# Memory attention of the prompt as two passes of seven Strassen products on pairs of tiles

## The chip, the cores and the metric

The program runs on one core of one Trainium2 chip. A core has TensorE (PE in the profile; the loading of its weights is listed as PEld), VectorE (DVE), ScalarE (ACT), GpSimd (POOL) and SyncE (SP), which issues most of the DMAs. Each engine takes its own instructions in order, and waits on semaphores for the others. The metric is device time in microseconds, the median of several runs: lower is better.

## The reference, cut to what matters

One layer of a streaming encoder. For the prompt (2048 rows of 1024 channels, float32) it does a mixer, then attention into 256 memory tokens, then a SwiGLU feed-forward. The middle one is what changes:

```python
def memory_attention(h, mk, mv, w_mq, w_mo):          # h = rmsnorm(x, g_mem_pre)
    q = (h @ w_mq).reshape(B, T, MEM_HEADS, MEM_HEAD_DIM)          # 4 heads of 256
    s = jnp.einsum("bthd,bmhd->bhtm", q, mk, ...) * (MEM_HEAD_DIM ** -0.5)
    p = jax.nn.softmax(s, axis=-1)
    o = jnp.einsum("bhtm,bmhd->bthd", p.astype(mv.dtype), mv).reshape(B, T, D_MODEL)
    return o @ w_mo
# x = x + rmsnorm(memory_attention(...), g_mem_post), then h = rmsnorm(x, g_ffn_pre)
```

The kernel folds the weights into the memory first: F1 = w_mq times the keys (1024 x 1024, its columns head by head) and F2 = values times w_mo (1024 x 1024). The attention of a row is then two products with 1024 x 1024 matrices, h F1 = scores and p F2 = output, with the softmax between them.

## The kernel before

Rows are worked in tiles of 128: prompt tiles 0 to 15, and tile 16 (`S_TILE`), the sample rows. The program is five stages, one after the other:

- `phase_mem`: norm of the memory tokens, keys and values, then F1 and F2, which are kept in DRAM (`f1s`, `f2s`).
- the projections, the convolution and the band attention (`phase_proj`, `attention`), which the change doesn't touch.
- `mixout`: output projection of the mixer, row tile by row tile, with memory attention of the sample rows (`cross_sample`) in between. The sum with the residual goes to DRAM as `x1[t]` (an addition on POOL, L1038, and a DMA that POOL issues, L1039).
- `phase_cross` (L1169): memory attention of the prompt.
- `gate_up` and `down`: the feed-forward, as seven Strassen products of 2 x 2 blocks. Row tiles are taken in pairs, whose seven row forms (sums and differences of half rows) lie in DRAM as `hn[g]`; `tform` loads and transposes them.

float32 products are made of three passes on PE: each operand is split into hi (rounded to fp32r, on ACT) and lo (the rest, on DVE or POOL), and hi·hi + hi·lo + lo·hi is summed. `mm3` issues the three passes for one bank of PSUM (512 columns), `mm3h` for two.

In `phase_cross` every tile t goes through `norm` (square sum on ACT, power on POOL, scaling on DVE, 8 transposes on PE, split), `scores` (8 blocks x 3 passes x 2 halves = 48 matmuls of 512 columns, then maximum, exponential, normalization), `probs` (8 transposes and the split of the probabilities) and `values` (48 matmuls, then `postnorm`). F1 and F2 are loaded and split once, at the start (`load`), and stay in SBUF. The loop interleaves `probs(t)`, `scores(t+1)`, `norm(t+2)`, `values(t)`. `natural(g, p)` reads two finished tiles back from `x2`, norms them and writes their seven row forms to `hn`; it runs from the fifth tile on, and for the last two pairs (`todo`) in `gate_up`.

The order of instructions on each engine is fixed when the program is built, by a scheduler that goes by its own estimate of durations, so what the text writes next to each other may stand apart on the engines. Buffers are fixed spots in three big tiles: `sbf` (float32), `sbr` and `sbx` (hi and lo), `psb` (PSUM); beside them lie `flexb` tiles, which take the place of tiles of an earlier stage. Such a tile can be written only when every use of the earlier tile at its place is over.

## Time and profile before

| | us |
|---|---|
| median of 3 runs (2915.76 to 2922.65) | 2921.47 |
| the profiled execution, its own time | 2912.2 |
| span of that profile | 2910.4 |
| up to the last matmuls of `mixout` | 0 to 1104 |
| memory attention of the prompt | 1104 to 1488 |
| gate and up products | 1488 to 2425 |
| down products | 2425 to 2910 |

The times of the stages are read from the order of PE's matmuls in the trace (a little of each stage runs inside the one before). A row of the groups gives line, engine, operation, output<-input, partitions x elements and count, then the busy time of the group, the mean duration of one in ns, and the idle time before it. A row of the windows gives a stretch of the span and, for each engine, its busy time in it and the number of instructions, then the clock granted to PE (1.00 is full), the busy share of the DMA engines and GB/s. A PE row of the timeline shows a run of matmuls; the last one ends 0.16 us after the next could start, since matmuls overlap.

### The profile page before, as it was taken

To read this page: it belongs to the slowest core of one execution; us is meant where nothing else is said; L and a number is where in the kernel's file an instruction comes from. 1 tells how busy PE (TensorE), PEld (TensorE's weight loads), DVE (VectorE), ACT (ScalarE), POOL (GpSimd) and SP (SyncE) were. 2 spreads that over 40 slices of the span, in tenths; PEclk is the share of its full clock that TensorE was granted. 3 is DMA by queue.
4 is the path that set the end of the run, shared out by engine and by line. 5 is a ranking of instruction groups with operands and counts; after the bars stand their busy time and mean duration, and the time that the engine had idled before them with its cause. 6 is when DMAs were issued, how large, how long until landed. Compare 5 with 4: busy or idle time off the path is not lost.

```text
span 2910.4 us, 44563 instructions
## 1 busy us (share of the span) xinstructions
PE 2859.6 (98%) x16248; PEld 2589.3 (89%) x16248; DVE 2081.8 (72%) x3053; ACT 1308.3 (45%) x2623; POOL 1400.0 (48%) x1298
## 2 busy tenths in 40 slices
PE   9999999999999999999999999999999999999998
PEld 9999999988877678888889999999999998888786
...
GB/s 292 247 95 201 82 168 113 207 233 211 220 109 199 257 196 151 51 156 71 181 194 145 130 111 137 196 151 157 124 171 127 149 138 258 212 174 226 233 211 143
DMA packets 200382, 496.81 MB, mean 171 GB/s; under 512 B 19257, under 2 KB 90809, under 8 KB 191322
## 3 DMA queue, kind: packets, MB, share of 16 engines
...
q14 instruction: 93, 0.76, 0.1%
...
## 4 chain that ended last, share of the span: by engine, by line
PE 81%; DVE 5%; DMA 5%; POOL 3%; issue 3%; ACT 2%; SPq 0%; DVEq 0%; POOLq 0%; ACTq 0%
PE psb L273 18%; PE psb L272 18%; PE psb L271 18%; PE psb L279 18%; DMA sbf<-in_w_down_dram 2%; PE psb L848 2%; PE psb L817 2%; PE psb L835 1%; POOL sbf L1479 1%; PE psb L1334 1%; DMA sbf<-x 1%; POOL flexb L515 1%; PE psb L1097 1%; DMA sbf<-in_x_prompt_dram 1%; DVE flexb L732 1%
## 5 line engine op out<-in xcount | busy, mean ns | idle before, releaser
L271 PE MATMUL psb<-sbr 128*128 128x384 f32 (+3 forms) x2672 | 915.2, 344 | 5.1 <-DVE sbf L1396 2.3
L272 PE MATMUL psb<-sbr 128*128 128x384 f32 (+3 forms) x2352 | 802.5, 341 | 0.3
L273 PE MATMUL psb<-sbr 128*128 128x512 f32 (+2 forms) x1712 | 609.1, 357 | 4.7 <-DVE sbr L1549 4.6
L271 PEld LDWEIGHTS psb<-sbr 128*128 128x128 f32 x2672 | 503.0, 188 | 40.5 <-DVE sbf L1396 2.6
L273 PE MATMUL psb<-sbr,sbx 128*128 128x384 f32 (+2 forms) x1484 | 474.5, 321 | 1.6 <-POOL sbx L266 1.6
L272 PEld LDWEIGHTS psb<-sbr 128*128 128x128 f32 x2352 | 443.6, 189 | 27.0 <-DVE sbr L321 0.9
L273 PEld LDWEIGHTS psb<-sbr 128*128 128x128 f32 x1712 | 321.0, 188 | 40.2 <-DVE sbr L1549 8.2
L1357 DVE TENSOR_TENSOR sbr<-sbf,sbr 128x512 fp32r<-128x512 f32 x258 | 258.1, 1003 | 48.2 <-ACT sbr L1356 45.0
L1356 ACT CAST sbr<-sbf 128x512 fp32r<-128x512 f32 x258 | 159.3, 620 | 292.3 <-PE psb L272 250.0
L273 PEld LDWEIGHTS psb<-sbr,sbx 128*128 128x128 f32 x1484 | 279.9, 189 | 1.9 <-POOL sbx L266 1.8
L505 DVE SCALAR_TENSOR_TENSOR psb<-sbf,psb 128x768 f32<-128x768 f32 (+1 forms) x290 | 264.4, 912 | 6.2
L279 PE MATMUL psb<-sbr 128*128 128x512 f32 x984 | 241.2, 395 | 1.4 <-DVE sbr L266 0.5
L1549 DVE TENSOR_TENSOR sbr<-sbf,sbr 128x384 fp32r<-128x384 f32 (+2 forms) x242 | 167.9, 716 | 96.7 <-ACT sbr L1548 94.1
L279 PEld LDWEIGHTS psb<-sbr 128*128 128x128 f32 x984 | 182.6, 189 | 45.2 <-issue 4.3
L1548 ACT CAST sbr<-sbf 128x384 fp32r<-128x384 f32 (+2 forms) x242 | 112.8, 483 | 174.0 <-PE psb L272 151.3
L266 POOL TENSOR_TENSOR sbx<-sbf,sbr 128x1024 fp32r<-128x1024 f32 (+1 forms) x62 | 152.0, 2455 | 79.1 <-ACT sbr L264 61.7
L1479 POOL TENSOR_TENSOR sbf<-sbf 128x512 f32<-128x512 f32 x77 | 106.9, 1394 | 172.4 <-DMA sbf<-in_w_down_dram 170.9
L279 PE MATMUL psb<-sbr,sbx 128*128 128x512 f32 x750 | 184.6, 394 | 1.7 <-ACT sbx L991 1.4
L515 POOL TENSOR_TENSOR flexb<-flexb,flexb 128x128 f32<-128x128 f32 (+1 forms) x180 | 170.2, 946 | 20.1 <-ACT flexb L514 10.5
L1357 DVE TENSOR_TENSOR sbx<-sbf,sbx 128x512 fp32r<-128x512 f32 x153 | 165.9, 1087 | 14.9 <-ACT sbx L1356 14.6
L279 PEld LDWEIGHTS psb<-sbr,sbx 128*128 128x128 f32 x750 | 138.7, 188 | 36.0 <-issue 4.5
L271 PE MATMUL psb<-sbr,sbx 128*128 128x384 f32 (+1 forms) x524 | 170.0, 326 | 0.2 <-ACT sbr L1336 0.2
(328 smaller groups left out, 5821.7 us busy)
## 6 DMA issues: line engine op xcount, KB each, us to landing
...
sbf<-in_w_gate_dram SPq DMA_DIRECT2D x66, 512.0 KB, 3.3
sbf<-in_w_up_dram SPq DMA_DIRECT2D x66, 512.0 KB, 3.4
...
sbf<-x SPq DMA_DIRECT2D x49, 512.0 KB, 3.9
sbf<-in_w_in_dram SPq DMA_DIRECT2D x48, 512.0 KB, 4.1
...
```

The source lines that it names most:

```text
L266: self.lo_engine.tensor_tensor(lo[:, c], wf[:, c], hi[:, c].bitcast(F32), ALU.subtract)
L271: nc.tensor.matmul(ps, lh, rh, start=start, stop=False, **kw)
L272: nc.tensor.matmul(ps, lh, rl, start=False, stop=False, **kw)
L273: nc.tensor.matmul(ps, ll, rh, start=False, stop=stop, **kw)
L279: nc.tensor.matmul(y[o], l, r[:, o * 512:(o + 1) * 512], start=start and x == 0, stop=stop and x == 2)
L505: nc.vector.scalar_tensor_tensor(acc if w < CW - 1 else o, src(w), cwt[:, j, w:w + 1], acc, ALU.mult, ALU.add)
L515: nc.gpsimd.tensor_tensor(o, o, v, ALU.add)
L1356: nc.scalar.copy(hs[j][:, :], src[j])
L1357: nc.vector.tensor_tensor(ls[j][:, :], src[j], hs[j][:, :].bitcast(F32), ALU.subtract)
L1479: nc.gpsimd.tensor_tensor(acc[:, :], acc[:, :], q[:, :], ALU.add if s > 0 else ALU.subtract)
L1548: nc.scalar.copy(ch[:, m], a[:, x, m])
L1549: nc.vector.tensor_tensor(cl[:, m], a[:, x, m], ch[:, m].bitcast(F32), ALU.subtract)
```

## The change

`phase_cross` now runs over pairs of tiles, (0,3), (1,4), (2,5), (6,9), (7,10), (8,11), (12,14), (13,15), twice: eight steps make the scores and probabilities of all tiles, which go to DRAM (`zs`), and eight more steps make the output rows. In each step the two tiles' rows (2 x 128 rows, 2 halves of 512 channels) and the matrix (2 x 2 blocks of 512 x 512) are multiplied by seven Strassen products of 4 blocks x 3 passes = 12 matmuls of 512 columns. The row forms are made in PSUM and SBUF after the transposes (`aforms`); the matrix forms come from DRAM. `phase_mem` writes F1 as its seven forms (`keep`, differences on POOL), with the gain `g_mem_pre` already in it; the forms of F2 are made in steps 1 and 4 of the first pass (`combine`, on POOL). The rows that a step finishes are normed for the feed-forward and written as row forms at once (`rows_out`, `forms_out`), so that `natural` is left for the sample pair and, in `gate_up`, for the last two pairs. `gate_up` has other spots for its buffers (3 for loaded row forms instead of 5, and 9 in its first group).

```diff
 phase_mem
+        def keep(h, fo, of):            # f1: seven forms, the halves of head pairs
+            c, sub = h % 2, nc.gpsimd.tensor_tensor
+            part = lambda j: self.fs[0][:, j, :, c * 256:(c + 1) * 256]
...
+            for j, t, x, y in ((4, t1, b12, b11), (3, t3, b22, b12), (1, t2, b22, t1), (5, t4, t2, b21)):
+                sub(t, x, y, ALU.subtract)
+                nc.sync.dma_start(part(j), t)
-                        nc.vector.tensor_copy(fo[:, ic, :], ps[:, :NM])
-                    nc.sync.dma_start(self.f1s[:, :, h, :], fo[:, :, :])
+                        nc.vector.tensor_scalar(fo[:, ic, :], ps[:, :NM], gk[:, ic:ic + 1], None, ALU.mult)
+                    keep(h, fo, of)
 phase_cross
-        fr = Joined(*self.flex(ctx, *[(1024, F32R)] * 11))
+        f6h, f6l, *fs, fq, f3, f4 = self.flex(ctx, *[(2048, F32R)] * 2, *[(1024, F32R)] * 3, (2048, F32), *[(1024, F32R)] * 2)
+        fs = [f3, f4] + fs
...
+        def bform(halves_, j, engine):  # two halves of form j: hi on ACT, lo on engine
+            for x in range(2):
+                wf, c = next(halves_), slice(2 * x, 2 * x + 2)
+                nc.scalar.copy(hi[:, c, :], wf[:, :, :])
+                engine.tensor_tensor(lo[:, c, :], wf[:, :, :], hi[:, c, :].bitcast(F32), ALU.subtract)
+        def combine(c):                 # f2: four loads, four differences, four stores
...
+            for j, t, x, y in ((4, b11, b12, b11), (3, b12, b22, b12), (1, b22, b22, b11), (5, b21, b22, b21)):
+                nc.gpsimd.tensor_tensor(t, x, y, ALU.subtract)
+                nc.sync.dma_start(part(j), t)
+        def aforms(src, out):           # 16 transposes, 7 splits, s1..s4 on DVE
+            p21, p22 = turn(xb, 0), turn(xb, 1)
+            nc.scalar.copy(a21, p21)
+            tt(s1, p22, a21, ALU.add)
+            p11, p12 = turn(xa, 0), turn(xa, 1)
+            split(p11, nc.vector)
+            tt(s2, s1, p11, ALU.subtract)
+            split(s2, nc.gpsimd)
+            split(p12, nc.vector)
+            tt(s3, p11, a21, ALU.subtract)
+            split(s3, nc.gpsimd)
+            split(s1, nc.gpsimd)
+            split(p22, nc.vector)
+            tt(s4, p12, s2, ALU.subtract)
+            split(s4, nc.gpsimd)
+        def product(bank, j, start):
+            (ah, al), (bh, bl) = af[j], bf[j]
+            for k in range(4):
+                self.mm3(bank, ah[:, k, :], al[:, k, :], bh[:, k, :], bl[:, k, :], start and k == 0, k == 3,
+                         skip_group_check=True)
+        def rows_out(y, x, t, parts, done):
+                nc.scalar.activation(junk[:, c], src, AF.Square, accum_out=ss[:, i:i + 1])
+                tt(y[:, c], src, gpost[:, c], ALU.mult)
+            stt(x[:, :], y[:, :], r[:, :], x[:, :], ALU.mult, ALU.add)
+            nc.sync.dma_start(self.x2[t], x[:, :])
+            r = self.rms(pool, x[:, :])
+            stt(y[:, :], x[:, :], r[:, :], gffn[:, :], ALU.mult, ALU.mult)
+        def forms_out(s, ys, xa):       # four differences of 512 on POOL, four stores to hn
...
+        for s in range(2 * n):          # n = 8; between(j) also runs the tails of older rows
+            product(a, 0, True)
+            nc.scalar.copy(yb[:, lo], a)
+            product(b, 1, True)
+            tt(ya[:, hi], yb[:, lo], b, ALU.add)
+            product(a, 2, False)
+            product(b, 3, False)
+            tt(yb[:, lo], yb[:, lo], b, ALU.add)
+            product(c, 4, True)
+            tt(yb[:, hi], yb[:, lo], c, ALU.add)
+            product(d, 5, True)
+            tt(yb[:, lo], yb[:, lo], d, ALU.subtract)
+            product(c, 6, False)
+            tt(ya[:, hi], ya[:, hi], c, ALU.add)
```

Three places show how the instructions moved. The first is POOL at the end of `mixout`, before the change, from the store of x1[13] on (L1038 the addition for x1, L1195 lo of F1, L1039 the store of x1):

```order
L1039 DMA x_13_50_122<-flexb_153 128x1024
L1034 TENSOR_TENSOR flexb_153<-flexb_153 128x1
L288 TENSOR_SCALAR flexb_153<-flexb_153 128x1
L289 TENSOR_TENSOR flexb_153<-flexb_153,mhalf_78 128x1
L1195 TENSOR_TENSOR sbr<-sbf,sbr 128x1024
L1038 TENSOR_TENSOR flexb_153<-flexb_153 128x1024
L1195 TENSOR_TENSOR sbr<-sbf,sbr 128x1024
L1039 DMA x_14_51_123<-flexb_153 128x1024
...
L1038 TENSOR_TENSOR flexb_153<-flexb_153 128x1024
L1039 DMA x_15_52_124<-flexb_153 128x1024
```

And POOL at the same place now (L1266 lo of a row form, L1224 lo of a matrix form, L1234 a difference of `combine`, L1059 the addition for x1, L1060 its store; flexb_9874 and flexb_9866 take the place of flexb_169, which holds the buffers of `mixout`):

```order
L1059 TENSOR_TENSOR flexb_169<-flexb_169 128x1024
L1266 TENSOR_TENSOR flexb_9890<-flexb_9882,flexb_9890 128x512
L1224 TENSOR_TENSOR sbr<-sbf,sbr 128x1024
L1060 DMA x_14_67_139<-flexb_169 128x1024
L1224 TENSOR_TENSOR sbr<-sbf,sbr 128x1024 x3
...
L1234 TENSOR_TENSOR sbf<-sbf 128x1024
L1059 TENSOR_TENSOR flexb_169<-flexb_169 128x1024
L285 TENSOR_SCALAR sbf<-sbf 128x1
L1060 DMA x_15_68_140<-flexb_169 128x1024
L286 TENSOR_TENSOR sbf<-sbf,mhalf_78 128x1
L1266 TENSOR_TENSOR flexb_9874<-flexb_9882,flexb_9874 128x512
L1224 TENSOR_TENSOR flexb_9866<-sbf,flexb_9862 128x1024 x2
```

What moved (with the rows left out): four lo of matrix forms, three lo of row forms and a difference of `combine`, which needs two loads of F2, now stand ahead of the last addition for x1; the lo of row form 6 and of matrix form 6 stand behind its store, in tiles that lie where that store's source lies.

The second is DVE in one tile of `phase_cross` before (L1259 is `natural`, L1212 the maximum, L1221 the normalization, L308 and L1231 lo of the rows and of the probabilities):

```order
L1231 TENSOR_TENSOR sbr<-psb,sbr 128x1024
L1259 SCALAR_TENSOR_TENSOR sbf<-sbf,flexb_9819 128x1024 x2
L1212 TENSOR_REDUCE sbf<-psb 128x4
L303 SCALAR_TENSOR_TENSOR sbf<-sbf 128x1024
L1219 RECIPROCAL sbf<-sbf 128x4
L1221 TENSOR_SCALAR sbf<-sbf 128x256 x4
L308 TENSOR_TENSOR sbr<-psb,sbr 128x1024
L328 SCALAR_TENSOR_TENSOR sbf<-psb,sbf 128x1024
```

And DVE in a part of one step of the second pass now (L1453, L1459, L1462, L1465 take sums out of PSUM; L1266, L1272, L1290 are `aforms` for the next step; L1326, L1332, L1338 are `rows_out`):

```order
L1453 TENSOR_TENSOR sbf<-sbf,psb 128x512
L1266 TENSOR_TENSOR flexb_9878<-psb,flexb_9878 128x512
L1290 TENSOR_TENSOR flexb_9882<-psb,flexb_9882 128x512
L1338 SCALAR_TENSOR_TENSOR sbf<-sbf,flexb_9858 128x1024
L1326 TENSOR_TENSOR sbf<-psb,sbf 128x512
L1266 TENSOR_TENSOR sbx<-psb,sbx 128x512
L1459 TENSOR_TENSOR sbf<-sbf,psb 128x512
L1462 TENSOR_TENSOR sbf<-sbf,psb 128x512
L1465 TENSOR_TENSOR sbf<-sbf,psb 128x512
L1326 TENSOR_TENSOR sbf<-sbf 128x1024
L1272 TENSOR_TENSOR flexb_9882<-psb,flexb_9882 128x512
L1332 SCALAR_TENSOR_TENSOR sbf<-sbf 128x1024
```

What moved: before, no matmul of the scores or of the output waited for an eviction in its own tile; now three evictions of each step (the copy of the first sum on ACT, L1453 and L1462) must be over before a product one place further on may add to the same bank, and they share DVE's queue with the rest.

332 lines of the change are left out of this document (221 added, 111 removed).

## Prediction

> **What bounds the kernel.** I read the page first (busy times, then the chain that ended last), then windows of the stage that changes, then PE's timeline in it, then the groups of DVE, POOL and ACT there.
>
> ```profile
> span 2910.4 us, 44563 instructions
> PE 2859.6 (98%) x16248; PEld 2589.3 (89%) x16248; DVE 2081.8 (72%) x3053; ACT 1308.3 (45%) x2623; POOL 1400.0 (48%) x1298
> PE 81%; DVE 5%; DMA 5%; POOL 3%; issue 3%; ACT 2%; SPq 0%; DVEq 0%; POOLq 0%; ACTq 0%
> ...
> core 0: us, PE busy (x) PEld busy (x) DVE busy (x) ACT busy (x) POOL busy (x), PEclk, DMA share, GB/s
> 1092.00:1488.00 396.00, 394.12 (x1895) 329.21 (x1894) 195.56 (x210) 138.40 (x290) 161.81 (x192) 1.00 0.37 126
> 1285.30:1308.90 23.60, 23.60 (x114) 19.72 (x113) 13.18 (x12) 8.31 (x18) 14.29 (x19) 1.00 0.43 155
> 1700.00:1800.00 100.00, 100.00 (x579) 100.00 (x578) 79.47 (x111) 37.78 (x68) 56.49 (x40) 1.00 0.32 116
> ```
>
> PE carries the chain. In the memory attention it is busy for 394.12 of 396.00 us, a tile takes 23.6 us, and DVE (13.18) and POOL (14.29) have two fifths of their time left even where `natural` runs. So a matmul less is time less there, as long as no other engine takes over. The last row is `gate_up` in its steady part: the same seven products, with DVE at 79% and PE never idle.
>
> **What is removed on PE.** The price of a matmul, from the timeline:
>
> ```profile
> 1288.36 6.96 PE L279 MATMUL psb<-sbr,sbx 128*128 128x512 f32 x30
> ...
> 1302.20 1.03 PE L306 MATMUL psb<-ident,sbf 128*128 128x128 f32 x8
> 1302.99 4.12 PE L279 MATMUL psb<-flexb,sbr 128*128 128x512 f32 x17
> ...
> 2450.00:2550.00 100.00, 100.00 (x443) 82.81 (x442) 52.35 (x68) 37.65 (x75) 40.28 (x30) 1.00 0.69 230
> ```
>
> 30 matmuls of 512 columns in 6.96 - 0.16 us are 0.227 us each; 8 transposes take 0.79 us, 0.10 each. In `down`, where the passes come from `mm3` as they now will, 443 in 100 us are 0.226: the order of the passes costs nothing. Before: 16 tiles x 96 = 1536 matmuls. Now 16 steps x 7 products x 12 = 1344, and as many transposes as before (16 a step). Removed: 192 x 0.227 = 43.6 us; a step is 84 x 0.227 + 16 x 0.10 = 20.7 us. The Trainium skill ("TensorE: Matmul & The Clock Gate", Back-to-back issue gap) gives about 131 ns for a sustained matmul of 512 columns; by that the saving would be an estimated 25 us. The trace has 0.227, so I keep 43.6.
>
> **What is added on the other engines in a step.**
>
> ```profile
> L837 DVE TENSOR_TENSOR sbx<-psb,sbx 128x512 fp32r<-128x512 f32 x80 | 53.9, 683 | 3.7 <-ACT sbx L836 3.1
> L1221 DVE TENSOR_SCALAR sbf<-sbf 128x256 f32<-128x256 f32 x44 | 27.1, 678 | 0.4
> L303 DVE SCALAR_TENSOR_TENSOR sbf<-sbf 128x1024 f32<-128x1024 f32 x12 | 21.9, 1822 | 37.6 <-POOL sbf L289 37.5
> L1259 DVE SCALAR_TENSOR_TENSOR sbf<-sbf,flexb 128x1024 f32<-128x1024 f32 x12 | 14.9, 1283 | 12.2 <-POOL sbf L1258 12.2
> L1212 DVE TENSOR_REDUCE sbf<-psb 128x4 f32<-128x1024 f32 x12 | 14.7, 1221 | 9.4 <-PE psb L279 9.4
> L329 POOL TENSOR_TENSOR sbf<-sbf 128x1024 f32<-128x1024 f32 x12 | 28.8, 2402 | 16.8 <-DVE sbf L328 16.8
> L1264 POOL TENSOR_TENSOR sbf<-sbf 128x512 f32<-128x512 f32 x6 | 13.6, 2265 | 0.0
> L289 POOL TENSOR_TENSOR sbf<-sbf,mhalf 128x1 f32<-128x1 f32 x24 | 13.4, 557 | 1.4
> L1260 POOL TENSOR_TENSOR sbf<-sbf 128x512 f32<-128x512 f32 x6 | 7.7, 1289 | 0.5
> L1216 ACT ACTIVATE sbf<-psb,sbf 128x256 f32<-128x256 f32 x48 | 22.1, 473 | 33.7 <-DVE sbf L1212 33.7
> L296 ACT ACTIVATE sbf<-sbf 128x1024 bf16<-128x1024 f32 x12 | 12.7, 1058 | 63.5 <-DMA sbf<-x 63.5
> L836 ACT CAST sbx<-psb 128x512 fp32r<-128x512 f32 x80 | 46.1, 586 | 7.0 <-PE psb L835 5.5 <-DVE flexb L732 0.7
> ```
>
> First pass, DVE: 12 operations on 512 columns from PSUM (five evictions, three lo, s1 to s4) x 0.683 = 8.2; maxima 2 x 1.22; normalization 8 x 27.1/44 = 4.9; in all 15.5 of 20.7 us. ACT: 9 copies x 0.586, 4 x 1.06 for norm and scaling, 8 x 0.47: 13.3. POOL: 4 lo x 1.29 and two powers: 6.3. All have room, so I put the pass at nothing; what hides it is PE's 20.7 us.
>
> Second pass, DVE: 13 x 0.683 = 8.9 from PSUM, and 5.5 thousand-column operations with both inputs in SBUF (L1326, L1332, L1338), at 1.283 (7.1) or, where POOL works beside them, at 1.822 (10.0): 16.0 to 18.9. POOL: 8 x 1.289 (four lo, four differences) and four powers, 12.5; at L1264's 2.265, 20.3. DVE stands between 77% and 91%; at 79% `gate_up` shows no loss. An eviction may be late by one product (2.7 us) before PE waits. I take 0.5 us a step, 4 us for eight; bounds 0 and, if only 79% of DVE can be had, 18.9 - 0.79 x 20.7 = 2.5 us a step, 20 us.
>
> **The start.**
>
> ```profile
> 1104.27 1.03 PE L306 MATMUL psb<-ident,sbf 128*128 128x128 f32 x8
> 1099.25 6.67 DVE L1195 TENSOR_TENSOR sbr<-sbf,sbr 128x1024 fp32r<-128x1024 f32 x2 [0.49 <-ACT sbr L1194]
> 1118.08 1.23 DVE L1195 TENSOR_TENSOR flexb<-sbf,sbx 128x1024 fp32r<-128x1024 f32 x1 [0.60 <-DMA x<-flexb]
> 1111.91 2.40 POOL L1038 TENSOR_TENSOR flexb<-flexb 128x1024 f32<-128x1024 f32 x1 [2.40 <-DVE flexb L1037]
> 1114.61 0.63 POOL L1039 DMA_DIRECT2D x<-flexb  x1 [0.30 <-POOL flexb L1038]
> 1128.39 1.19 PE L279 MATMUL psb<-sbr 128*128 128x512 f32 x4 [0.40 <-ACT sbr L1230]
> 1131.05 1.09 PE L306 MATMUL psb<-ident,sbf 128*128 128x128 f32 x8 [1.47 <-DVE sbr L1231]
> sbf<-f1s SPq DMA_DIRECT2D x8, 512.0 KB, 4.7
> ```
>
> Before, the places of `mixout`'s buffers came free at 1118.08, after the addition for x1[15] (ends 1114.3) and its store (3.4 us); only F2 lay there, and PE lost 0.40 + 1.47 us. Now row forms 5 and 6 and matrix form 6 lie there. PE ends `mixout` at 1104.3, starts the first step there, and has five products done after 5 x 2.72 us and some 20 transposes, at about 1120. The addition for x1[15] stands on POOL behind four lo of matrix forms (2.40 each), three of row forms (1.29), and a difference of `combine`. That one waits for a block of F2, whose place is free only when half a matrix form has been loaded (4.7 us) and split. From 1098.8 (24 matmuls before 1104.3, when the output weights in form 2's place have been used): the second half of form 2 is done at 1105, its place reloaded and split by 1112, F2 there at 1117, the difference at 1119.5, the addition at 1122, the store at 1126. With DVE and POOL in each other's way (two lo took 6.67 us instead of 2.45 beside POOL's) it is nearer 1129. So PE waits 6 to 9 us; I take 8, and 1 for the clock that follows a stall, less the 1.9 of before: +7. Bounds -2 (no wait) and +12.
>
> **Between the passes.** 14 loads and splits of F2's forms (ACT 1.06 each, as L296; DVE 8 x 1.23, POOL 6 x 2.40) fall into 2 x 20.7 us, each form due one step after its place is free, so there is room. But the loads (4.7 us, as f1s) stand in DVE's queue ahead of evictions: one that comes late costs PE up to 4.7 - 2.7 = 2 us. I take two of these: +4; bounds 0 and, for all eight of DVE's, 16.
>
> **The end of the stage, and the first stage.**
>
> ```profile
> 1520.00:1540.00 20.00, 20.00 (x117) 19.96 (x116) 17.58 (x22) 9.30 (x18) 13.87 (x13) 1.00 0.42 159
> 1540.00:1560.00 20.00, 14.43 (x82) 13.82 (x80) 19.86 (x18) 5.33 (x10) 19.28 (x16) 1.00 0.55 201
> 1560.00:1580.00 20.00, 18.98 (x102) 18.98 (x103) 17.41 (x23) 6.17 (x11) 10.95 (x8) 0.91 0.51 188
> ...
> 50.00:60.00 10.00, 9.69 (x79) 9.29 (x78) 8.92 (x17) 3.15 (x3) 0.00 (x0) 1.00 1.02 346
> 60.00:70.00 10.00, 10.00 (x85) 10.00 (x84) 6.56 (x11) 6.49 (x10) 1.35 (x3) 1.00 1.00 338
> 70.00:80.00 10.00, 10.00 (x86) 10.00 (x85) 8.91 (x13) 5.02 (x8) 1.33 (x2) 1.00 0.61 208
> ```
>
> At the start of `gate_up` DVE (19.86 of 20) and POOL (19.28) are full, PE loses 5.6 + 1.0 us, and the clock falls to 0.91. The work there stays: 21 row forms to turn, the first weights, two `natural`. The forms can now be split only as the last step frees their places, and the loads stand behind the stores of x2 on SP; but two products of the next block may run ahead. +1; bounds -7 (the stall goes) and +10. In the turns between groups, three load places instead of five: the forms wait for the products that free their places, so nothing; at most one load, 3 us, at each.
>
> `phase_mem` writes 14 half megabytes of F1 instead of 8: 3.1 MB, at 338 GB/s 9.3 us of a DMA that is already full from 50 to 70 us. Weights are loaded three ahead, and from 70 to 80 the DMA has 39% free. The eight differences on POOL (2.40 each, 19 us) stand where POOL is idle, but their stores stand in SP's queue between the loads of weights, one every 2.4 us for a weight every 2.8 (24 matmuls at 10/85 us): just enough. +2; bounds 0 and 9. `natural` leaves the stage for six pairs, whose rows are no longer read back; zs adds 8 MB out and in; at 0.43 DMA share both are hidden.
>
> **The sum.** -43.6 + 4 + 7 + 4 + 1 + 2 = -25.6 us. The profiled execution took 2912.2, so 2886.6 by it; the median of the runs shown is 9.3 us higher. I take the difference off the median: 2896.
>
> **Rivals.** A, all of it is hidden: only the 43.6 counts, 2878. For it: `gate_up` runs so at 79% of DVE. Against: the order on POOL at the start.
>
> B, slower: DVE and POOL block each other in the second pass. The row for it is 1822 ns against 1283, and the 6.67 us for two lo. If each of the six SBUF operations waits for a whole difference (2.265), DVE needs 16.0 + 6 x 2.265 = 29.6 us a step, 8.9 over PE's: +71 over eight steps in place of the 4, about 2963. It decides from 24.4 us a step on: (43.6 - 14)/8 = 3.7 over. Against: POOL has only eight such operations for six of DVE's, and `gate_up` mixes them as densely. The Trainium skill ("SBUF — State Buffer", Who interferes with whom) has this rule: a DVE instruction with two SBUF inputs and a GpSimd instruction that reads SBUF block each other for their whole length; by that rule and the trace's 1822 the effect is there, and only its size is open.
>
> C, the pile-up at the start and between the passes is twice what I took, and the first stage pays its 9: -43.6 + 4 + 14 + 8 + 1 + 9 = -8, 2914, no change that can be told.
>
> **Chances.** The forecast (2887 to 2906) 0.47, A and near it (2872 to 2887) 0.18, between forecast and C (2906 to 2912) 0.11, C and what is within 0.3% (2913 to 2930) 0.11, B or a sum of stalls beyond that 0.13. A measurement of this kernel tells 0.3%, 8.8 us, from no change: faster 0.76, same 0.11, slower 0.13. The range 2877 to 2922 leaves out most of B and the edge of A.
>
> **What would show it.** PE instructions down by 192 matmuls; steps of 20.7 us with no idle PE in the first pass (a wait on L1453 or L1462 would show A wrong); a wait of PE for `flexb` at about 1120, ended by ACT after x1[15]'s store; in the second pass DVE at 80 to 90%, SBUF operations of 1.3 to 1.8 us; PE's idle time near 1430 still some 7 us. The prediction fails if the steps of the second pass are above 22 us, or PE stands still in the first 110 us.

## The result, and the profile after

The changed kernel took 2917.93 us, the median of 20 runs (2914.59 to 2923.57); the kernel before, 2917.48 in 20 runs beside it. The ratio is 1.0001 with a 95% interval of 0.9994 to 1.0008: no difference. 25.6 us less were forecast, so 26 us of gain are missing. (The forecast of 2896 started from a median of three executions that lies 4 us above that of the 20.) One execution of e1 below took 4375 us at a granted clock of 0.59 and is left out of its ratio. The page of the changed kernel, first the span, then busy times, then the chain that ended last:

```profile
span 2912.8 us, 44818 instructions
PE 2835.8 (97%) x16056; PEld 2559.9 (88%) x16056; DVE 2172.3 (75%) x3232; ACT 1383.4 (47%) x2779; POOL 1506.3 (52%) x1339
PE 75%; DVE 7%; DMA 7%; issue 4%; POOL 4%; ACT 2%; SPq 0%; DVEq 0%; POOLq 0%; ACTq 0%
```

The 192 matmuls are gone (16056 instructions of PE for 16248), but PE's busy time is only 23.8 us shorter, not 43.6, and its share of the chain fell from 81% to 75%: PE waits, and at times runs slower. The windows show where. First the kernel before, from the end of `mixout`'s last matmul (1104.4) to 1600 us, when `gate_up` runs steadily; then the changed kernel, from its end of `mixout` (1114.7). The columns are length, busy time with instructions of PE, PEld, DVE, ACT and POOL, PE's clock, DMA share and GB/s.

```profile
1104.40:1140.00 35.60, 33.73 (x161) 27.63 (x160) 23.73 (x28) 18.04 (x34) 5.72 (x9) 1.00 0.52 174
1140.00:1480.00 340.00, 340.00 (x1629) 284.16 (x1628) 156.08 (x167) 109.38 (x238) 143.05 (x176) 1.00 0.33 115
1480.00:1600.00 120.00, 111.09 (x643) 108.96 (x642) 100.79 (x125) 49.33 (x92) 76.75 (x65) 0.99 0.47 170
```

```profile
1114.70:1140.00 25.30, 16.26 (x57) 11.46 (x56) 15.58 (x14) 14.12 (x23) 23.84 (x18) 0.73 0.68 230
1140.00:1200.00 60.00, 60.00 (x291) 49.55 (x288) 42.38 (x67) 41.47 (x95) 41.75 (x42) 1.00 0.50 170
1200.00:1260.00 60.00, 54.10 (x250) 43.54 (x249) 44.62 (x71) 31.11 (x76) 28.31 (x26) 1.00 0.60 204
1260.00:1300.00 40.00, 40.00 (x195) 33.45 (x194) 31.33 (x50) 22.06 (x50) 14.39 (x10) 1.00 0.35 119
1300.00:1340.00 40.00, 37.91 (x182) 30.96 (x181) 36.54 (x48) 26.75 (x54) 27.88 (x19) 1.00 0.76 263
1340.00:1420.00 80.00, 80.00 (x387) 66.79 (x386) 60.49 (x72) 34.59 (x70) 60.12 (x63) 1.00 0.67 234
1420.00:1520.00 100.00, 88.72 (x440) 74.65 (x439) 78.53 (x95) 45.08 (x88) 55.92 (x61) 0.97 0.64 221
1520.00:1600.00 80.00, 76.19 (x431) 75.58 (x430) 67.84 (x85) 29.64 (x55) 57.23 (x46) 0.98 0.53 181
```

Three losses lie here: the start (57 instructions in 25.3 us, where the second pass does 387 in 80.00, so about 13.5 us lost; before, 1.9 idle), a place in the first pass (5.9), and the end of the stage with the start of `gate_up` (15.1 idle and 4.6 of clock; before, 8.9 and 1.2). Between the passes 2.1 us are lost, and in the second pass none: 387 instructions in 80.00 us are a step of 20.7 us, as forecast.

The fourth loss lies before the stage. The attention stage's first matmul comes at 615.1 us instead of 607.6, and in proj the first transposes of `conv_norm` already come at 312.3 instead of 304.8. `phase_mem` lost 7.5 us, and the changed kernel's windows show where:

```profile
50.00:60.00 10.00, 9.06 (x74) 8.66 (x72) 9.33 (x13) 3.16 (x4) 5.78 (x3) 1.00 0.99 349
60.00:70.00 10.00, 7.15 (x45) 6.95 (x46) 8.64 (x11) 2.26 (x3) 9.92 (x4) 0.83 0.89 271
```

Its timeline there, of PE, DVE and POOL (start, length, engine, line, operation, out<-in, count, and in brackets the idle time before and what ended it):

```profile
60.53 0.39 PE L268 MATMUL psb<-sbr 128*128 128x256 f32 x1 [1.43 <-DVE flexb L436]
63.83 0.58 PE L268 MATMUL psb<-sbr 128*128 128x256 f32 x1 [2.32 <-DVE flexb L436]
...
56.66 3.42 DVE L263 TENSOR_TENSOR sbx<-sbf,sbr 128x1024 fp32r<-128x1024 f32 x1
60.39 2.98 DVE L263 TENSOR_TENSOR sbx<-sbf,sbr 128x1024 fp32r<-128x1024 f32 x1
...
56.59 5.71 POOL L401 TENSOR_TENSOR flexb<-flexb 128x1024 f32<-128x1024 f32 x2
```

DVE's splits of weights take 3.42 and 2.98 us while POOL subtracts, and PE waits for evictions that stand behind them. That looks like the cause; e7 below shows that it isn't.

At the start the chain is this, on PE, DVE and ACT:

```profile
1120.93 0.79 PE L268 MATMUL psb<-sbr,sbx 128*128 128x512 f32 x1 [5.21 <-ACT sbx L1265]
...
1110.87 1.41 DVE L1058 SCALAR_TENSOR_TENSOR flexb<-psb,flexb,sbf 128x512 f32<-128x512 f32 x2 [5.82 <-DMA x<-flexb]
1112.20 10.03 DVE L1224 TENSOR_TENSOR sbr<-sbf,sbr 128x1024 fp32r<-128x1024 f32 x4
1122.15 0.68 DVE L1266 TENSOR_TENSOR sbx<-psb,sbx 128x512 fp32r<-128x512 f32 x1
...
1117.24 1.99 ACT L1223 CAST sbr<-sbf 128x1024 fp32r<-128x1024 f32 x2 [5.01 <-DMA sbf<-f1s]
1120.29 1.07 ACT L1265 CAST sbx<-psb 128x512 fp32r<-128x512 f32 x2
```

PE waits for the first product, not for the sixth: for row form 0. ACT casts it at 1120.29, behind casts of matrix forms whose load came late, and DVE splits it at 1122.15, behind four splits of matrix forms. Those stood behind L1058 of `mixout`, which waited 5.82 us for the store of the row before, since `po` has one place. And the matmuls that follow are slow ones. The first and the last of nine in a row on PE's timeline:

```profile
1123.48 0.63 PE L268 MATMUL psb<-sbr,sbx 128*128 128x512 f32 x1
...
1126.89 0.63 PE L270 MATMUL psb<-sbr,sbx 128*128 128x512 f32 x1
```

They are 3.41 us apart for eight steps, 0.43 each, where the step sums of the stage have 0.23. Of the 13.5 us, PE stands idle for 9.0 (25.30 - 16.26); the other 4.5 are such slow matmuls.

In the first pass, DVE, POOL and PE in step 4, where `combine` makes its differences:

```profile
1221.05 7.24 DVE L1315 TENSOR_SCALAR sbf<-sbf 128x256 f32<-128x256 f32 x4
...
1220.57 7.30 POOL L1234 TENSOR_TENSOR sbf<-sbf 128x1024 f32<-128x1024 f32 x3
...
1214.13 0.50 PE L268 MATMUL psb<-sbr,flexb 128*128 128x512 f32 x1 [2.02 <-ACT sbf L1310]
1228.93 0.50 PE L268 MATMUL psb<-sbr,sbx 128*128 128x512 f32 x1 [2.25 <-DVE sbf L1469]
```

Four scalings of the softmax, 1.13 us in e2's row below, last as long as POOL's three subtractions, and the eviction behind them (L1469) is late: it ends at 1228.88, and PE had been ready since 1226.68 (1228.93 - 2.25). With scalings of 1.13 us it would have been over by 1222.8, by this sum from the rows. The Trainium skill ("SBUF — State Buffer", Who interferes with whom) says that such scalings too can take the port that DVE shares with GpSimd, and that the later one then stands still for the whole instruction; the trace agrees: the first three scalings end at 1223.11, 1225.58 and 1228.02, each about 0.15 us after a subtraction (1222.96, 1225.43, 1227.87).

At the end of the stage, PE:

```profile
1478.45 0.44 PE L268 MATMUL psb<-sbr 128*128 128x384 f32 x1 [2.25 <-ACT sbr L1544]
1488.72 0.63 PE L1522 MATMUL psb<-ident,sbf 128*128 128x128 f32 x4 [0.82 <-DMA sbf<-hn]
...
1510.06 0.44 PE L269 MATMUL psb<-sbx,sbr 128*128 128x384 f32 x1 [2.04 <-DVE sbx L1525]
1565.00 0.44 PE L268 MATMUL psb<-flexb,sbr 128*128 128x384 f32 x1 [3.81 <-DVE flexb L1595]
```

Late weights, late rows and late splits alternate, each short.

### The profile page after: what moved, and what is told of

It reads as the page before. It is cut to its first block, busy times and chain, and to the rows that moved or that the text cites. A ratio compares the mean times of both kernels' runs of the same rounds, so it can differ in the third digit from the quotient of the medians.

```text
span 2912.8 us, 44818 instructions
## 1 busy us (share of the span) xinstructions
PE 2835.8 (97%) x16056; PEld 2559.9 (88%) x16056; DVE 2172.3 (75%) x3232; ACT 1383.4 (47%) x2779; POOL 1506.3 (52%) x1339
## 4 chain that ended last, share of the span: by engine, by line
PE 75%; DVE 7%; DMA 7%; issue 4%; POOL 4%; ACT 2%; SPq 0%; DVEq 0%; POOLq 0%; ACTq 0%
PE psb L270 21%; PE psb L268 21%; PE psb L269 21%; PE psb L276 5%; PE psb L869 2%; PE psb L838 2%; PE psb L856 1%; DMA sbf<-in_w_down_dram 1%; POOL sbf L1667 1%; DMA sbf<-x 1%; DVE psb L526 1%; DVE sbr L1545 1%; DMA sbf<-hn 1%; PE psb L1522 1%; PE psb L1118 1%
## 5 line engine op out<-in xcount | busy, mean ns | idle before, releaser
L268 PE MATMUL psb<-sbr 128*128 128x384 f32 (+3 forms) x2812 | 959.3, 344 | 12.8 <-DVE flexb L436 3.8
L269 PE MATMUL psb<-sbr 128*128 128x384 f32 (+3 forms) x2644 | 898.7, 340 | 0.2
L268 PEld LDWEIGHTS psb<-sbr 128*128 128x128 f32 x2812 | 530.0, 189 | 50.9 <-ACT sbr L1736 5.2
L269 PEld LDWEIGHTS psb<-sbr 128*128 128x128 f32 x2644 | 499.5, 189 | 27.0 <-DVE sbr L318 0.4
L270 PE MATMUL psb<-sbr,sbx 128*128 128x384 f32 (+3 forms) x1400 | 459.0, 329 | 2.6 <-POOL sbx L263 1.6
L1545 DVE TENSOR_TENSOR sbr<-sbf,sbr 128x512 fp32r<-128x512 f32 x360 | 354.9, 988 | 52.5 <-ACT sbr L1544 51.7
L270 PEld LDWEIGHTS psb<-sbr 128*128 128x128 f32 x1852 | 347.8, 188 | 39.3 <-DVE sbr L1737 7.1
L270 PEld LDWEIGHTS psb<-sbr,sbx 128*128 128x128 f32 x1400 | 266.0, 190 | 9.9 <-POOL sbx L263 1.8
L1667 POOL TENSOR_TENSOR sbf<-sbf 128x512 f32<-128x512 f32 x77 | 104.7, 1366 | 167.9 <-DMA sbf<-in_w_down_dram 159.4
L268 PE MATMUL psb<-sbr,sbx 128*128 128x384 f32 (+2 forms) x440 | 155.6, 354 | 8.8 <-ACT sbx L1265 6.6
L261 ACT CAST sbr<-sbf 128x1024 fp32r<-128x1024 f32 x98 | 102.1, 1049 | 119.9 <-PE psb L269 83.6
L1539 POOL TENSOR_TENSOR sbf<-sbf 128x512 f32<-128x512 f32 x66 | 94.4, 1430 | 113.8 <-DVE sbr L1545 71.6
L269 PE MATMUL psb<-sbr,sbx 128*128 128x384 f32 (+2 forms) x416 | 145.3, 349 | 0.0
L535 ACT ACTIVATE flexb<-sbf 128x128 f32<-128x128 f32 (+1 forms) x180 | 104.0, 585 | 69.7 <-POOL flexb L536 64.1
L269 PE MATMUL psb<-sbx,sbr 128*128 128x512 f32 (+2 forms) x376 | 134.6, 359 | 2.3 <-DVE sbx L1525 2.0
```

The lines of the kernel that those rows point to most:

```text
L268: nc.tensor.matmul(ps, lh, rh, start=start, stop=False, **kw)
L269: nc.tensor.matmul(ps, lh, rl, start=False, stop=False, **kw)
L270: nc.tensor.matmul(ps, ll, rh, start=False, stop=stop, **kw)
L1545: nc.vector.tensor_tensor(ls[j][:, :], src[j], hs[j][:, :].bitcast(F32), ALU.subtract)
L1667: nc.gpsimd.tensor_tensor(acc[:, :], acc[:, :], q[:, :], ALU.add if s > 0 else ALU.subtract)
```

## The experiments

The theory after this look: POOL's long subtractions hold up DVE in `phase_mem` and `combine`, and the order of work on DVE and ACT holds up the start. The rivals: bytes and SP's queue; DVE that simply has too much; loads that come late. All edits are against the changed kernel, but for e15. The table gives, from the profiles, the first matmul of the attention stage (A), the end of `mixout` (M) and the last transposes of `gate_up`'s second turn (G), in us, then the median time and its ratio to the kernel before, run on the same chip. A, M and G come from one profile each. Where `phase_mem` is that of the changed kernel (changed, e2, e3, e5, e6, e11, e13, e14), A lies between 613.7 and 615.8; from A to M, where the edits change little, the rows have 496.0 to 502.5 us; and from M to G, the five rows whose edits change nothing behind M (e1, e6, e7, e8, e9) have 1076.2 to 1079.7, the changed kernel 1077.7 and the kernel before 1083.7. Smaller differences say nothing by themselves.

| kernel | A | M | G | median | ratio, 95% interval |
|---|---|---|---|---|---|
| before | 607.6 | 1104.4 | 2188.1 | 2917.48 | |
| changed | 615.1 | 1114.7 | 2192.4 | 2917.93 | 1.0001 (0.9994 to 1.0008) |
| e1_mem_dve | 613.7 | 1109.7 | 2185.9 | 2914.56 | 1.0002 (0.9987 to 1.0016) |
| e2_comb_dve | 615.8 | 1114.0 | 2185.4 | 2910.74 | 0.9985 (0.9975 to 0.9996) |
| e3_start_first | 615.6 | 1117.7 | 2199.6 | 2922.65 | 1.0027 (1.0015 to 1.0038) |
| e4_three | 612.8 | 1111.4 | 2186.6 | 2912.18 | 0.9983 (0.9971 to 0.9994) |
| e5_two_po | 614.4 | 1113.8 | 2185.4 | 2911.64 | 0.9985 (0.9976 to 0.9995) |
| e6_natural_late | 614.5 | 1115.8 | 2192.4 | 2915.92 | 0.9999 (0.9989 to 1.0009) |
| e7_no_diff | 616.3 | 1118.8 | 2197.1 | 2919.47 | 1.0005 (0.9993 to 1.0016) |
| e8_mem_act | 617.4 | 1117.9 | 2197.6 | 2918.14 | 1.0011 (1.0000 to 1.0023) |
| e9_few_stores | 612.1 | 1109.4 | 2188.7 | 2917.52 | 0.9996 (0.9986 to 1.0006) |
| e10_mem_comb_po | 615.7 | 1113.4 | 2178.6 | 2904.38 | 0.9951 (0.9937 to 0.9965) |
| e11_wf_places | 613.7 | 1111.2 | 2190.9 | 2920.46 | 1.0009 (0.9998 to 1.0020) |
| e12_four | 614.8 | 1112.8 | 2180.1 | 2905.99 | 0.9959 (0.9945 to 0.9973) |
| e13_five_nat | 615.0 | 1112.9 | 2181.9 | 2908.71 | 0.9967 (0.9954 to 0.9980) |
| e14_split_pool | 615.5 | 1113.8 | 2185.3 | 2912.58 | 0.9980 (0.9970 to 0.9990) |
| e15_before_stores | 615.0 | 1112.0 | 2195.3 | 2923.62 | 1.0026 (1.0013 to 1.0040) |
| e16_four_best | 612.2 | 1111.8 | 2174.3 | 2895.34 | 0.9924 (0.9911 to 0.9938) |
| e17_five_best | 613.2 | 1113.8 | 2179.9 | 2905.87 | 0.9961 (0.9948 to 0.9974) |

### The first stage: e1, e7, e8, e9, e15

```diff
 # e1 (and e8): in keep
-            c, sub = h % 2, nc.gpsimd.tensor_tensor
+            c, sub = h % 2, nc.vector.tensor_tensor
```

> The eight differences of F1 that phase_mem makes are computed by DVE instead of POOL; loads, stores and their order on SP stay. Theory 1 (DVE's splits of weights, which read and write SBUF only, stand still while POOL subtracts): DVE's splits of 128x1024 go from 2.98-3.42 us back to 1.2, PE's waits of 1.43 and 2.32 us at 60 and 64 us and the low clock behind them go, and the first matmul of the attention stage comes at 608 to 611 us instead of 615.1; the whole kernel 3 to 6 us faster. Theory 2 (the stores of the differences hold up the weights' loads on SP, or the DMA is full): the attention stage begins at 613 to 617 and the time stays.

A comes at 613.7: 1.4 us of 7.5, no more than the spread of A between profiles. DVE's splits are short again (1.22 us), and PE now waits 2.79 us at 63 us, because DVE is busy for 10.00 of 10 us with the subtractions. M is 5.0 us earlier; 3.6 of them fall into stages that the edit doesn't touch, where the profiles differ by as much without an edit. The time shows no gain.

```diff
 # e7: no differences, all stores
-                sub(t, x, y, ALU.subtract)
-                nc.sync.dma_start(part(j), t)
+                nc.sync.dma_start(part(j), x if j == 4 else b22 if j == 3 else y if j == 5 else b12)
```

> phase_mem leaves out the eight differences of F1 and stores the blocks themselves in their places, so the attention's scores are made of other forms; loads and stores are as many as in the changed kernel. If the arithmetic of the differences costs the time of the first stage, on POOL by holding up DVE and on DVE (e1) by its own ten us, the attention stage begins at 608 to 610 us instead of 615.1, and all is 5 to 7 us faster. If the fourteen stores and their place in SP's queue cost it, it begins at 612 to 616.

This decides on the arithmetic. Without any difference, on any engine, A comes at 616.3, no earlier than with them. The waits at 60 and 64 us are gone, and others stand in their place (0.79 at 55 us, 0.46 to 0.74 at 92 to 106, 3.34 at 121). The DMA is full through it (also 1.02 from 50 to 60 us):

```profile
60.00:70.00 10.00, 10.00 (x88) 10.00 (x86) 9.17 (x14) 5.01 (x10) 1.57 (x2) 1.00 1.08 383
70.00:80.00 10.00, 9.81 (x81) 9.37 (x80) 7.56 (x12) 6.19 (x11) 0.74 (x2) 1.00 1.03 373
```

```diff
 # e8: e1, and
-                        nc.vector.tensor_scalar(fo[:, ic, :], ps[:, :NM], gk[:, ic:ic + 1], None, ALU.mult)
+                        nc.scalar.activation(fo[:, ic, :], ps[:, :NM], AF.Copy, scale=gk[:, ic:ic + 1])
```

> In phase_mem the eight differences are on DVE, and the 32 scaled evictions of F1 (0.48 us each, 15 us on DVE) are on ACT. If DVE's total in that stretch is the limit once POOL no longer blocks it, the attention stage begins at 608 to 611 us, and all is 4 to 7 us faster than the changed kernel. If ACT, which also casts the weights, becomes the limit or the stores are, it begins at 612 to 616.

617.4: taking work from DVE does not help either. ACT now has the evictions, and PE waits 2.94 us for one of them at 59.8, so this run alone would not tell DVE's load from ACT's.

```diff
 # e9: in keep only j == 4 is stored, without a difference; raw reads blocks 0, 2, 6 in place of 1, 3, 5
-                sub(t, x, y, ALU.subtract)
-                nc.sync.dma_start(part(j), t)
+                if j == 4:
+                    nc.sync.dma_start(part(j), x)
```

> phase_mem leaves out the differences of F1 and stores only 8 half megabytes of F1 (4 MB, as before the change) instead of 14; the first pass then reads the blocks 0, 2, 6 again for the forms that were left out, so the scores are made of other forms. Since without the differences but with all stores the attention stage began at 616.3 us, the bytes and their places in SP's queue are suspected: by that it begins at 607 to 610 us (607.6 before the change). If it begins at 613 or later, neither the arithmetic nor the bytes of F1 are the cause, but the scaled evictions or the other places of the buffers.

612.1, between the two forecasts, and the time shows no gain. The first transposes of `conv_norm` come at 307.7 instead of e7's 313.8: six stores less are 6.1 us there. Of what is left to before's 304.8, a wait of 2.19 us at 58.6 is a new one: the scheduler moved a norm of proj ahead into `phase_mem`.

```diff
 # e15: the kernel before
                     nc.sync.dma_start(self.f1s[:, :, h, :], fo[:, :, :])
+                    for x in range(3 if h > 1 else 0):
+                        nc.sync.dma_start(self.f1x[:, 3 * (h - 2) + x, :, :256], fo[:, :4, :])
```

> The kernel before the change, with six more stores of half a megabyte in phase_mem (to a place that nothing reads), three behind each of the last two heads: the bytes of F1 that the change adds, without its differences. If the bytes and the places in SP's queue make the first stage's loss, the attention stage begins at 612 to 616 us instead of 607.6, and all is 5 to 8 us slower than before. If not, it begins at 607 to 610 and the time stays within 3 us.

The kernel before, with six stores added and nothing else, begins the attention stage at 615.0 and is 0.26% slower, 6.7 us. Its windows and PE show how: the DMA is full from 70 to 80 us too, and PE waits for a weight (the cast on ACT, L264).

```profile
70.00:80.00 10.00, 5.73 (x48) 5.52 (x47) 3.37 (x5) 3.67 (x7) 1.62 (x3) 0.99 1.01 373
80.03 0.58 PE L271 MATMUL psb<-sbr 128*128 128x256 f32 x1 [4.30 <-ACT sbr L264]
```

So 3.1 MB more through a DMA that is full are enough for the loss of the first stage: 7.4 us at A. At the transposes of `conv_norm` e15 is 6.1 us late (310.9 for 304.8), as much as e9 gave back, where the changed kernel is 7.5 late. In the changed kernel the waits carry other names (DVE's evictions), and e1 and e7 show that they do not set the end: without POOL's subtractions it comes earlier by no more than the profiles differ by.

### combine: e2

```diff
 # in combine
-                nc.gpsimd.tensor_tensor(t, x, y, ALU.subtract)
+                nc.vector.tensor_tensor(t, x, y, ALU.subtract)
```

> The eight differences of F2 in the first pass (combine) are computed by DVE instead of POOL. Theory 1 (blocking): the four scalings of the softmax at 1221 us take 1.1 us again instead of 7.24, PE's waits of 2.25 and 0.84 us behind them go; the wait of 2.02 us before, which ends with ACT (held by a late row block), stays. 2 to 4 us faster. Theory 2 (DVE simply has too much in that step, and POOL is innocent): DVE's additional 10 us put the same or a longer wait there, 0 to 5 us slower.

Here the blocking counts. In e2's window PE is busy throughout:

```profile
1200.00:1260.00 60.00, 60.00 (x290) 49.88 (x289) 46.18 (x85) 34.98 (x88) 19.52 (x23) 1.00 0.58 204
```

On its DVE's timeline the differences take 1.23 us each, and the scalings 1.13:

```profile
1217.19 2.46 DVE L1234 TENSOR_TENSOR sbf<-sbf 128x1024 f32<-128x1024 f32 x2
1223.22 1.13 DVE L1315 TENSOR_SCALAR sbf<-sbf 128x256 f32<-128x256 f32 x4
```

The wait of 2.02 us that I had put down to a late row went too; its cause stays open. G is 7.0 us earlier (0.7 of them at M), the time 0.15% under the kernel before. But the edit did two things: on e2's DVE the eviction L1469 (at 1219.58) also stands ahead of the four scalings, where it stood behind them. Theory 2 is out, since DVE's additional work cost PE nothing; that the blocking made the wait of 2.25 us rests on the sum above, and the share of the changed order in the gain is not measured.

### The start: e3, e4, e5

```diff
 # e3
         gen = aforms(src.pop(0), af)
-        next(gen)
-        next(gen)
+        with self.tc.high_priority(offset=HP):
+            next(gen)
+            next(gen)
```

> The first two parts of the row forms of step 0 are given priority, so that ACT and DVE split form 0 before they split the matrix forms that wait for their loads. Theory 1 (order alone makes the start late): PE begins the first product within 1.5 us of the end of mixout (it waited 5.21 and 0.74 us), the clock stays up, and the later waits of 1.38, 0.61 and 1.11 us are at most 2 us together; 7 to 11 us faster. Theory 2 (the matrix forms themselves are late, since their places come free late and POOL and DVE take 2.4 us each): the wait moves to products 1 to 4, at most 3 us are won.

The first product begins at once, and then PE stands still for 12.83 us, longer than before, ahead of the transposes of step 1: their rows are loaded behind loads of F1 whose places DVE frees late. Row form 0 was only the first thing that DVE's delay reached.

> The three edits together. Theory 1 throughout: 12 to 20 us faster than the changed kernel, 2898 to 2906, and the kernel before is beaten by 0.4 to 0.7 per cent. If only the first stage counts: 3 to 6 us faster, no difference from the kernel before.

e4 is e1, e2 and e3 together: 0.17% under the kernel before. The wait at the start is 12.31 us there.

```diff
 # e5: in mixout
-            po = self.t(pool, [P, D], F32, "po")
+            po = self.t(pool.at("po", 4, (ff, [5, 26])) if i == len(order) - 3 else pool, [P, D], F32, "po")
```

> The last three rows of mixout get two places for the result (po) in turn instead of one; the order of the instructions on every engine is the same as in the changed kernel. There DVE waited 5.82 us at 1105 for the store of x1[13], with the splits of the matrix forms and of row form 0 behind it. Theory 1 (that wait makes the start late): DVE goes on at once, PE's wait ahead of the first product falls from 5.21 us to at most 2, the low clock of the first matmuls goes, and the kernel is 5 to 9 us faster. Theory 2 (the splits themselves are slow, 10.03 us for four beside POOL, or the loads behind them): at most 2 us.

The order on all engines is the same, only the place differs. L1058 runs at 1104.51 without a wait, and the first product waits 1.40 us instead of 5.21, with its matmuls 0.23 us apart behind the first three; the second product, 3.54 instead of 1.38. The last row is the window from M to 1140 us:

```profile
1104.51 1.40 DVE L1058 SCALAR_TENSOR_TENSOR flexb<-psb,flexb,sbf 128x512 f32<-128x512 f32 x2
1105.83 4.58 DVE L1224 TENSOR_TENSOR sbr<-sbf,sbr 128x1024 fp32r<-128x1024 f32 x2
...
1116.20 0.50 PE L268 MATMUL psb<-sbr,sbx 128*128 128x512 f32 x1 [1.40 <-ACT sbx L1265]
1123.46 0.50 PE L268 MATMUL psb<-sbr,sbx 128*128 128x512 f32 x1 [3.54 <-ACT sbx L1265]
...
1113.80:1140.00 26.20, 19.11 (x84) 14.42 (x81) 11.68 (x15) 16.15 (x30) 21.31 (x20) 0.93 0.70 244
```

G is 7.0 us earlier (0.9 of them at M), the time 6.3 us under the changed kernel. The store of x1[13] made the first product late. At 0.207 us an instruction, 8.8 us are lost up to 1140 instead of 13.5, and of the 4.7 won only 1.9 are idle time (7.1 instead of 9.0): the rest is the clock. What is left is put down to DVE's splits at 2.3 us each; no run tests that.

### The end of the stage: e6, e11, e13, e14

```diff
 # e6
-                    if g == 0 and x == 1 and self.todo:
+                    if g == 0 and x == 1 and fp > 2 and self.todo:
 # e11
-.at("wf", 4, (sbF, [24, 28, 34.5, 38.5]))
+.at("wf", 4, (sbF, [42.5, 46.5, 24, 28]))
 # e13
-.at("s", 2, (sbF, [14, 20, 22])).at("nat", 2, (sbF, [8, 10, 12]))
+.at("s", 2, (sbF, [46.5, 20, 22])).at("nat", 2, (sbF, [8, 10, 12, 14, 48.5]))
 # e14
-                nc.vector.tensor_tensor(ls[j][:, :], src[j], ...
+                (nc.gpsimd if f < 3 and j % 2 else nc.vector).tensor_tensor(ls[j][:, :], src[j], ...
```

> The two calls of natural that remain in gate_up come three pairs of weight blocks later. Theory 1 (POOL's differences of natural and of the weights, together with DVE's 21 splits of the forms, make PE's wait of 3.8 us at 1561 and the clock of 0.91 behind it): that wait goes, 3 to 5 us faster, and nothing comes in its place, since DVE is at 77 to 79% later on. Theory 2 (the splits and the weights' differences alone do it): 0 to 1 us.

> The first weights of gate_up are loaded to the places of y of the last step but one, and the second weights to those that took the first, so that both loads can start earlier; natural's nt moves to 34.5. Theory 1 (late weights make PE's waits of 2.25 us at 1478 and 2.04 us at 1510): these go, and the waits for hn (0.5 to 1.1 us each) stay; 2 to 5 us faster. Theory 2 (DVE's queue of splits is the limit from 1470 to 1510 and the weights wait in it anyway): 0 to 1 us.

Neither wins time, but neither settles its theory. In e6 `natural` did not move: the order of work on PE, DVE, ACT and POOL is that of the changed kernel, and POOL makes the first difference of the last pair in both at the same place (first the changed kernel, then e6):

```profile
1543.63 1.66 POOL L1380 TENSOR_TENSOR sbf<-sbf 128x512 f32<-128x512 f32 x1 [0.84 <-DVE sbf L1379]
1543.65 1.66 POOL L1380 TENSOR_TENSOR sbf<-sbf 128x512 f32<-128x512 f32 x1 [0.84 <-DVE sbf L1379]
```

So the built kernel has `natural` where it was, though the program's text calls it later. PE still waits, 3.84 us at 1565, and what `natural` costs there is not tested. In e11 the weights' loads start earlier (the first at 1460.2 instead of 1468.4), and yet PE waits 3.49 us at 1475.5 for the cast of the first weights, where it waited 2.25: other places for the weights bring nothing.

> gate_up gets five load places for the rows that are turned (nat) instead of three, as before the change; one place of s moves. Theory 1 (the rows come too late, PE's waits for hn of 0.5 to 1.3 us, six of them between 1438 and 1500, 4.4 us together): those waits go, and the last transposes of the second turn come 3 to 6 us earlier (2192.4 in the changed kernel). Theory 2 (DVE, with 16 to 18 of 20 us, is late with its splits, and the rows wait for it): the waits change their releaser to DVE or ACT, 0 to 1 us.

G comes 10.5 us earlier (1.8 of them were there at M), and the time is 9.2 us under the changed kernel. PE's waits for rows from 1470 to 1500 are down to one (0.25 us at 1487.83), and two short waits for DVE's splits take their place:

```profile
1473.39 0.66 PE L1522 MATMUL psb<-ident,sbf 128*128 128x128 f32 x4 [1.19 <-DVE sbr L1525]
1480.37 1.25 PE L1522 MATMUL psb<-ident,sbf 128*128 128x128 f32 x8 [1.41 <-DVE sbr L1525]
```

The change had taken two of the five load places away. At the first turn between groups, near 1850, PE's waits fall from 1.87 us to 0.25. Some of the rest lies where the edit changes nothing: from 1200 to 1260 PE stands idle for 3.5 us here and for 5.9 in the changed kernel's profile.

> For the first three blocks of gate_up's weights every other split of a weight form (9 of 21) is on POOL instead of DVE. Theory 1 (DVE's queue is the limit from 1470 to 1570): PE's waits of 2.04 us at 1510 and 3.81 us at 1565 become shorter, 2 to 5 us faster. Theory 2 (POOL and DVE hold each other up, so that what DVE no longer does it loses by standing still): no change, or up to 4 us slower.

5.4 us under the changed kernel, so DVE's queue counts too, as long as the rows are late. The wait of 3.81 us is gone; one of 3.31 us at 1537.1, also for DVE, is there instead.

### Together: e10, e12, e16, e17

> Three edits together: differences of F1 and of F2 on DVE, two places for po. Alone they brought the last transposes of gate_up's second turn forward by 6.5, 7.0 and 7.0 us. If the losses are separate and add up, that point comes at 2172 to 2177 instead of 2192.4, and all takes 2898 to 2905, 0.4 to 0.6% less than before the change. If each only uncovers the next wait at the end of the stage, it comes at 2182 to 2186, and all takes 2907 to 2911.

2904.38, 0.49% under the kernel before and 13.5 us under the changed kernel. G comes 13.8 us earlier, where e1, e2 and e5 alone make 6.5, 7.0 and 7.0. Of e1's 6.5, 5.0 are there at M. From M to G, e2 takes 6.3 us less than the changed kernel, e5 6.1 and e10 12.5: the start and `combine` are separate losses that add up, and e1 adds nothing that shows.

> The edits of e10 and e11 together. If the losses add up: 2895 to 2902. If the end of the stage takes the gain: 2905 to 2911.

e12 is e10 with e11: 2905.99, no better than e10. The weights' places give nothing here either.

> e10 (differences of F1 and F2 on DVE, two places for po) together with e13 (five load places for the rows that gate_up turns). Alone they took 2904.4 and 2908.7 us, where the changed kernel takes 2917.9. If the end of the stage gives its 9 us on top of e10's 13: 2894 to 2898, 0.65 to 0.8% less than before the change. If both won the same wait: 2902 to 2906.

e16 is e10 with e13: 2895.34 us, 22.6 under the changed kernel and 0.76% under the kernel before (0.62 to 0.89%). It beats both. Its span is 2893.4 us; from its `mixout` on, the same windows:

```profile
1111.80:1140.00 28.20, 21.34 (x90) 16.43 (x89) 15.48 (x17) 17.91 (x29) 21.85 (x20) 0.88 0.70 240
...
1200.00:1260.00 60.00, 60.00 (x289) 49.84 (x289) 43.80 (x79) 32.81 (x83) 17.37 (x17) 1.00 0.53 192
```

At the start PE does 90 instructions in 28.2 us; at the 0.207 us of the second pass (80.00 / 387) they are worth 18.6, so 9.6 us are lost there instead of 13.5. The first pass is full. From M to G e16 takes 15.2 us less than the changed kernel, where e10 and e13 make 12.5 and 8.7. Counted on the timelines, by 1600 us e16 has done 633 of `gate_up`'s matmuls of 384 columns, the changed kernel 536 and the kernel before 559.

> e16 and e14 together (every other split of the first three blocks of weights on POOL). Alone e14 won 5 us. If DVE's queue is still the limit there once the rows come in time: 2889 to 2895. If not: as e16, or up to 3 us slower through the two engines holding each other up.

With e14's edit on top the time is 10.5 us longer. What won 5 us while the rows were late costs 10 once they come in time. In the groups of `gate_up`'s weight splits from 1460 to 1600 us (L1545), DVE does 48 splits in 68.1 us, 1.42 each, where in e16 it did 61 in 71.0, 1.16 each. But that mean hides one split. DVE, POOL and PE of e17:

```profile
1514.09 11.28 DVE L1545 TENSOR_TENSOR sbr<-sbf,sbr 128x512 fp32r<-128x512 f32 x1
...
1513.77 1.30 POOL L1380 TENSOR_TENSOR sbf<-sbf 128x512 f32<-128x512 f32 x1
...
1522.95 1.27 POOL L1386 TENSOR_TENSOR sbf<-sbf 128x512 f32<-128x512 f32 x1
...
1526.48 0.69 PE L268 MATMUL psb<-flexb,sbr 128*128 128x384 f32 x1 [9.98 <-DVE flexb L1595]
```

One split, 0.68 us where POOL is idle, stands still for 11.28 us while POOL runs eight subtractions in a row: four of `natural`, three of the weights' differences and one of the splits that the edit moved there. PE waits 9.98 us for an eviction behind it. Without that split the mean is 1.21. e16 has one of 5.37 us at 1519.8 in the same way.

## Why the prediction was wrong

"So a matmul less is time less there, as long as no other engine takes over": the first half held. 192 matmuls went, and a step of the second pass takes 20.7 us. The sum failed at the places around the steps; each of its terms, as forecast and as measured:

| term | forecast | measured | from |
|---|---|---|---|
| 192 matmuls | -43.6 | -43.6 | steps of 20.7 us |
| first pass | 0 | +5.9 | 60.00 - 54.10 |
| second pass | +4 | 0 | 80.00 of 80.00 |
| start | +7 | +11.6 | 13.5 - 1.9 |
| between the passes | +4 | +2.1 | 40.00 - 37.91 |
| end, start of `gate_up` | +1 | +9.6 | 15.1 + 4.6 - 8.9 - 1.2 |
| `phase_mem` | +2 | +7.5 | 615.1 - 607.6 |

- **The first stage.** The step "Weights are loaded three ahead, and from 70 to 80 the DMA has 39% free" failed. I had the price, 9.3 us for 3.1 MB, as an upper bound, and hid most of it in one window of ten us. The DMA's free time there was a short gap in a stage that is full on both sides. e15 has the price: 7.4 us for the stores alone.
- **The first pass.** "All have room, so I put the pass at nothing" failed. DVE's sum of busy times was right: from 1260 to 1300 it has 31.33 of 40.00 us. POOL's sum left out `combine`, whose four differences (4 x 2.40 = 9.6 us, in two of the steps) stand in no term. And POOL's 7.30 us without a break hold up DVE for more than two and a half of PE's products (2.72 each), which no sum over a step shows. I weighed the blocking in the second pass only, where rival B had it.
- **The second pass.** Rival B was wrong in its place. From 1340 to 1420 DVE is at 60.49 of 80.00 us, 76%, under the 80 to 90% that I gave. The operations of a thousand columns take 1.28 (L1332) to 1.81 us (L1338) there, as long as I had said; rival B wanted each of them to wait for a whole difference, 2.265 us more, and they don't:

```profile
L1338 DVE SCALAR_TENSOR_TENSOR sbf<-sbf,flexb 128x1024 f32<-128x1024 f32 x8 | 14.5, 1810 | 0.3 <-POOL sbf L286 0.3
```

- **The start.** "So PE waits 6 to 9 us" for row forms 5 and 6 was near in size (9.0 idle) and wrong in place. The wait for `flexb` after x1[15]'s store that I named did not come as the first wait. I followed POOL's queue to the addition for x1[15], and not DVE's, where L1058 waits for the store of the row before. That stall stood in the trace of before too (4.74 us at 1087.05), with nothing urgent behind it; the change put the first forms there.
- **The clock.** "1 for the clock that follows a stall" failed, and by more than any other term; the sum had nothing else for slow matmuls. At the start alone the slow matmuls cost 4.5 us. Counted from M to G over every matmul of both traces, at 0.227, 0.173, 0.147 and 0.109 us for 512, 384, 320 and 128 columns, the work is 44.0 us less; PE stands idle for 34.2 us instead of 11.5, and its matmuls take 22.1 us more than these prices instead of 7.0. So the waits cost 22.7 us, and the slow matmuls behind them another 15.
- **The end.** "In the turns between groups, three load places instead of five: ... so nothing; at most one load, 3 us, at each" failed: I costed it for the turns, and most of it came at the first filling, where 21 rows are wanted at once (1.3 us at the first turn). e13 prices it: 9.2 us.

By its own list: the count of matmuls and the steps of 20.7 us came; idle PE in the first pass, PE standing still for 1.43 and 2.32 us in the first 110 us and the wait on the first product each spoke against it. The wait for `flexb` at about 1120 did not come. PE's idle time at the end of the stage, forecast as "still some 7 us", was 15.1. Rival C was nearest: 2914, no change that can be told, with the start at twice my term (14, measured 11.6) and the first stage at 9 (7.5). It lacked `combine`, the end and the clock, so its total was near by luck. The measured terms make -6.9 us, and 2.8 more are lost between A and M, where profiles differ by more without an edit; G shows +4.3. The 8 us that the table lacks are in the count above: the table has some 8 of the 15 us of slow matmuls (4.5 at the start, 4.6 - 1.2 at the end), the others lie behind the shorter waits, and 1.3 are idle time at the first turn. The first matmul behind a wait of the rows above takes 0.34 us (0.50 - 0.16) where the next ones take 0.23.

One bound was worked out wrong: 18.9 us of DVE at 79% of the time need 23.9 us a step, 3.2 more than PE's 20.7, so 26 us over eight steps and not 20. Nothing hung on it.

That e16 takes what I forecast, 2895 for 2896, is no confirmation of my sum: it has four edits that I did not foresee to be needed (one of them, e1's, with no gain that shows), and still pays the 3.1 MB. By the same count from M to G, PE is idle for 23.1 us in e16 and its matmuls take 18.1 us more than the prices, so more than half of the loss behind M is still there.
